# Decay steps of a gated DeltaNet projection stage: other delays between them, and VectorE's and ScalarE's parts kept in program order

## The chip, the cores and the metric

The kernel runs on one core of a Trainium2 chip. The engines of a core work side by side, each through its own queue of instructions in order: TensorE (PE, with its weight loads as PEld), VectorE (DVE), ScalarE (ACT), GpSimd (POOL), and SyncE (SP), which here only issues DMA transfers. The metric is the device time of one execution in microseconds. Three runs of the kernel before took 2248.15, 2249.53 and 2255.58 us; the median is 2249.53.

## The reference

The program is a two-layer encoder trunk over two groups of tokens, 1024 and 256, with a model width of 1024. Layer 0 is two-dimensional neighbourhood attention, layer 1 a bidirectional gated DeltaNet, and a final RMSNorm follows. The change lies in layer 1. After the projection, a five-tap centred depthwise convolution and SiLU, it computes for each of 8 heads and both directions:

```python
g = jnp.cumsum(g.transpose(0, 2, 1).reshape(b, h, n, c), axis=-1)
diff = g[..., :, None] - g[..., None, :]
decay = jnp.where(tril, jnp.exp(jnp.where(tril, diff, 0.0)), 0.0)
k_beta = k * beta[..., None]
a_kk = jnp.where(tril_strict, jnp.einsum('bhncd,bhnsd->bhncs', k_beta, k) * decay, 0.0)
lhs = jnp.eye(c, dtype=jnp.float32) + a_kk
w = lax.linalg.triangular_solve(lhs, k_beta * jnp.exp(g)[..., None], left_side=True,
                                lower=True, unit_diagonal=True)
```

The decay is the exponential of a difference of two cumulative gates, masked to one triangle. It scales the products of keys of a chunk, and the triangular matrix that results has to be inverted.

## The kernel before

The kernel works on chunks of 128 tokens (NB = 10 of them), keeps two 32-bit parts of each projected operand, and so needs three matmuls for a product (`mm<-xh,wh`, `mm<-xl,wh`, `mm<-xh,wl` at L1250). The stage of the change runs from about 770 to 1595 us.

TensorE's main work in it is 32 blocks of 128 channels of q, k and v (L539 copies the result to `raw`) and the blocks of the gate z. A channel block is three PSUM blocks of 512, 512 and 256 tokens with 24 matmuls each, in a pool `mm` of three banks. Each channel block starts a side chain `conv`: ScalarE scales the raw block (L509), VectorE adds four taps (L512, the first kept in program order), ScalarE takes the SiLU (L518, kept in program order; `th`), and SP spills the result. `raw` has two buffers. A z block has a tanh on ScalarE (L563) and one multiplication on VectorE (L554), which frees its bank.

Once a head's k is there, the side chain `invert` of that head begins. In order: TensorE's products of the keys (`pk`, L641); VectorE's norms and the scaling of B (L645 to L649); ScalarE and VectorE take out the diagonal 32x32 blocks into D; VectorE inverts them by substitution (L665 to L673, 60 small operations); two transposes (L677 and L678); ScalarE copies the blocks to M (L686, L687, shown as `X<-D` and `X<-N`) while POOL fills W and WT (L692 to L694). Then there are two rounds in which blocks are joined: L703 on TensorE, L706 on ScalarE, L710 on TensorE, the copies of L712 to L718 on VectorE and ScalarE (two of them transposes into WT), L723, L726, L731 and L733, and SP spills W.

The matrix B of a head, which `invert` starts from, comes from a further side chain, `decays` (L614 to L626). It works on the ten chunks in groups of four, four and two. For each group and each of the two directions a matmul (L605) spreads the cumulative gates into a PSUM bank `t` (three buffers, shared with `pk`), VectorE adds the chunk's other gate and the mask for each chunk (L608, the "taps"), and ScalarE takes the exponential in place (L611). The group's tile E has one buffer. SP spills it to `e_dram` (L624) and POOL adds the two directions into B (L625). The next group's taps can write E only when the spill has read it. `decays` of the next head is put on the list of side chains from within `invert`, after the copies to WT.

The order of the work comes from two places. A side chain is a generator; a list (`Side`) counts the columns that the projection's matmuls have issued, and a chain is taken a step further when its own count is reached: `yield 3500` means 3500 columns later. That sets the order in the program. From it a scheduler makes each engine's queue, and may move instructions ahead of others, except those that `keep_in_program_order` ties. ScalarE has one table of functions loaded at a time; the exponential and the SiLU are in different tables, and `ACT_TABLE_LOAD` stands where it has to be changed.

## Time and profile before

| | |
|---|---|
| median of three runs | 2249.53 us (2248.15 to 2255.58) |
| the profiled execution | 2251.55 us, span 2249.7 us, granted TensorE clock 0.98 |
| TensorE busy | 2166.0 us |
| VectorE busy | 1509.2 us |
| ScalarE busy | 1146.6 us |
| POOL busy | 585.1 us |

The times of the profile count from the start of the span. Rows of a timeline give start, duration, engine, line, operation and tiles, and in brackets how long the engine was idle before it and what ended that. A row of waits gives the waiting engine and line, what it waited for, and the total, the count and the longest. Rows of windows give a stretch and its length, busy time and instructions of PE, PEld, DVE, ACT and POOL, the granted clock, the share of the DMA engines and GB/s.

### The profile page before, as it was taken

To read this page: it belongs to the slowest core of one execution; us is meant where nothing else is said; L and a number is where in the kernel's file an instruction comes from. 1 tells how busy PE (TensorE), PEld (TensorE's weight loads), DVE (VectorE), ACT (ScalarE), POOL (GpSimd) and SP (SyncE) were. 2 spreads that over 40 slices of the span, in tenths; PEclk is the share of its full clock that TensorE was granted. 3 is DMA by queue.
4 is the path that set the end of the run, shared out by engine and by line. 5 is a ranking of instruction groups with operands and counts; after the bars stand their busy time and mean duration, and the time that the engine had idled before them with its cause. 6 is when DMAs were issued, how large, how long until landed. Compare 5 with 4: busy or idle time off the path is not lost.

```text
span 2249.7 us, 34012 instructions
## 1 busy us (share of the span) xinstructions
PE 2166.0 (96%) x12502; PEld 1881.3 (84%) x12502; DVE 1509.2 (67%) x3370; ACT 1146.6 (51%) x2313; POOL 585.1 (26%) x631
## 2 busy tenths in 40 slices
PE   8999999999999999899999999999899999999998
PEld 7789989989878877788888888888788888877887
DVE  5577777776773858768577676867566666675444
ACT  6455545555673454454544546354456666654333
POOL 2100100110230422233132313231176766600000
PEclk9999999999999999899999999999899999999999
DMA  5424342533556343443534444442675566567322
GB/s 181 112 74 118 82 118 75 125 93 97 151 150 182 98 114 89 141 127 101 159 105 134 111 136 115 128 145 71 209 207 164 168 186 180 154 216 234 107 96 85
DMA packets 148456, 300.10 MB, mean 133 GB/s; under 512 B 44976, under 2 KB 67632, under 8 KB 147264
## 3 DMA queue, kind: packets, MB, share of 16 engines
q1 hardware_dynamic: 126784, 232.89, 32.7%
q0 software_dynamic: 12096, 44.05, 11.2%
q10 hardware_dynamic: 9408, 20.98, 3.0%
q8 instruction: 99, 1.62, 0.3%
q14 instruction: 69, 0.57, 0.1%
HBM read 211.92 MB, written 75.45 MB: 128 GB/s over the span
## 4 chain that ended last, share of the span: by engine, by line
PE 70%; DVE 17%; ACT 5%; DMA 4%; issue 3%; POOL 1%; SPq 0%; ACTq 0%; DVEq 0%; POOLq 0%
PE mm L1250 42%; PE mm L1266 4%; DVE tmp L671 3%; DVE X L673 3%; PE k L1014 3%; PE o L986 2%; PE k L1005 2%; PE O L263 2%; PE o L1027 2%; PE u L986 2%; DVE acc L512 2%; PE pt L243 2%; DMA yt<-y_spill 1%; PE t L940 1%; PE S L286 1%
## 5 line engine op out<-in xcount | busy, mean ns | idle before, releaser
L1250 PE MATMUL mm<-xh,wh 128*128 128x512 f32 (+1 forms) x1920 | 700.6, 365 | 6.3 <-DVE z L554 3.2
L1250 PE MATMUL mm<-xh,wl 128*128 128x512 f32 (+1 forms) x1920 | 700.7, 365 | 3.4 <-DMA wl<-w_o 2.2
L1250 PE MATMUL mm<-xl,wh 128*128 128x512 f32 (+1 forms) x1920 | 701.9, 366 | 0.3 <-DVE xl L352 0.2
L1250 PEld LDWEIGHTS mm<-xh,wh 128*128 128x128 f32 x1920 | 367.6, 191 | 52.8 <-DVE z L554 3.8
L1250 PEld LDWEIGHTS mm<-xh,wl 128*128 128x128 f32 x1920 | 367.5, 191 | 47.6 <-DMA wl<-w_o 2.6
L1250 PEld LDWEIGHTS mm<-xl,wh 128*128 128x128 f32 x1920 | 367.7, 191 | 43.1 <-DVE xl L352 0.4
L512 DVE SCALAR_TENSOR_TENSOR acc<-raw,cw,acc 128x1282 f32<-128x1282 f32 x128 | 199.1, 1555 | 4.7 <-ACT acc L509 2.3
L1202 ACT ACTIVATE wh<-wraw 128x1024 fp32r<-128x1024 f32 x92 | 96.8, 1055 | 139.2 <-PE mm L1250 112.7
L1200 POOL CAST wh<-wraw 128x1024 fp32r<-128x1024 f32 x32 | 34.2, 1070 | 498.2 <-PE mm L1250 441.4
L1250 PE MATMUL mm<-yh,wh 128*128 128x512 f32 (+1 forms) x384 | 137.5, 359 | 2.4 <-ACT yh L1124 2.2
L1250 PE MATMUL mm<-yh,wl 128*128 128x512 f32 (+1 forms) x384 | 137.0, 358 | 1.2 <-DVE wl L1204 1.2
L1250 PE MATMUL mm<-yl,wh 128*128 128x512 f32 (+1 forms) x384 | 137.6, 360 | 0.1
L1018 DVE TENSOR_TENSOR vl<-k,vh 128x256 fp32r<-128x256 f32 x160 | 67.1, 424 | 69.6 <-ACT vh L1017 65.1
L247 ACT ACTIVATE ph<-pt 128x512 fp32r<-128x512 f32 (+2 forms) x144 | 67.6, 479 | 77.0 <-PE pt L243 65.3
L539 ACT ACTIVATE raw<-mm 128x512 f32<-128x512 f32 (+1 forms) x96 | 49.9, 522 | 101.9 <-PE mm L1250 96.1
L248 DVE TENSOR_TENSOR pl<-pt,ph 128x512 fp32r<-128x512 f32 (+2 forms) x144 | 75.2, 538 | 38.2 <-ACT ph L247 36.7
L608 DVE SCALAR_TENSOR_TENSOR E<-t,lbG,mask 128x128 f32<-128x128 f32 x160 | 46.9, 342 | 79.7 <-DMA e_spill<-E 78.8
L1206 ACT ACTIVATE wl<-wraw 128x1024 fp32r<-128x1024 f32 x84 | 88.5, 1053 | 16.3 <-DMA wraw<-w_qk 8.4
L221 ACT ACTIVATE P<-P,mx 128x384 f32<-128x384 f32 (+1 forms) x128 | 75.0, 587 | 39.6 <-DVE mx L220 38.3
L1266 PE MATMUL mm<-wh,xl 128*128 128x256 f32 x320 | 91.9, 287 | 0.6 <-POOL xl L65 0.6
L1017 ACT ACTIVATE vh<-k 128x256 fp32r<-128x256 f32 x160 | 60.6, 380 | 62.5 <-PE k L1014 59.3
L1266 PE MATMUL mm<-wl,xh 128*128 128x256 f32 x320 | 91.6, 286 | 0.5 <-DVE wl L1204 0.5
(314 smaller groups left out, 4917.1 us busy)
## 6 DMA issues: line engine op xcount, KB each, us to landing
wraw<-w_qkv SPq DMA_DIRECT2D x32, 512.0 KB, 3.7
qkv_spill<-th SPq DMA_DIRECT2D x32, 512.0 KB, 2.7
wraw<-w_go SPq DMA_DIRECT2D x32, 512.0 KB, 3.6
wl<-w_qkv POOLq DMA_DIRECT2D x30, 512.0 KB, 8.0
Al<-e_spill SPq DMA_DIRECT2D x8, 1280.0 KB, 6.7
qe<-eg_spill SPq DMA_DIRECT2D x16, 640.0 KB, 8.0
wraw<-w_qk SPq DMA_DIRECT2D x16, 512.0 KB, 3.9
wl<-w_qk POOLq DMA_DIRECT2D x16, 512.0 KB, 8.6
```

The lines of the kernel that those rows point to most:

```text
L221: nc.scalar.activation(Pv, Pv, AF.Exp, scale=-1.0, bias=mx[:, 0:1], accum_out=mx[:, 1:2])
L247: nc.scalar.activation(view(ph), view(pt), AF.Copy)
L248: nc.vector.tensor_sub(view(pl), view(pt), view(ph))
L512: tap = nc.vector.scalar_tensor_tensor(acc, r[:, i:i + m], cw[:, f, i:i + 1], acc, op0=OP.mult, op1=OP.add)
L671: nc.vector.tensor_mul(tv, N[:, 0:c, c:c + 1].to_broadcast([128, c, n]), X[:, c:c + 1, c + 1:32].to_broadcast([128, c, n]))
L673: nc.vector.tensor_add(X[:, 0:c, c + 1:32], X[:, 0:c, c + 1:32], tv)
L986: self.tc.nc.tensor.matmul(ps, w[x], v[y], start=(first and i == 0), stop=(i == 2))
L1014: nc.tensor.matmul(pw, W[:, d, cs[d]], Y[d], start=True, stop=True)
L1202: nc.scalar.activation(wh, raw, AF.Copy)
L1206: nc.scalar.activation(wl, raw, AF.Copy, scale=-1.0)
L1250: nc.tensor.matmul(ps, w[:, k, :], x[k][b], start=(k == 0 and i == 0), stop=(k == KD - 1 and i == 2))
L1266: nc.tensor.matmul(ps, x[k][b][:, cc], w[:, k % 4, :], start=(k == 0 and i == 0), stop=(k == KD - 1 and i == 2))
```

## The change

`decay` becomes a generator: the matmul and VectorE's taps are its first step, and the exponential follows 2500 columns later. For all heads but the first, the taps and the exponential are tied in program order. In `decays` the delay after a direction is 3000 columns instead of 3500 (1000 for head 0), and after the spill of the first and the second group there is a further delay of 14000 columns (0 for head 0). In `invert` of head 0, the decays of head 1 are put on the list before the substitution, with a delay of 30000, rather than behind the copies to WT; for heads 1 to 6 the place and the delay of 4000 stay. The delay before L703's matmuls is 42000 columns for head 0, and 34000 as before for the others.

```diff
--- before.py
+++ after.py
@@ -599,16 +599,22 @@
         nc.vector.tensor_scalar(mask[:, d], a["jp"], 0.0, NEG, op0=drop, op1=OP.mult)
 
 
-def decay(nc, a, ap, pool, h, d, c0, n, E, nt=2):
-
+def decay(tc, a, ap, pool, h, d, c0, n, E, nt=2):
+
+    nc = tc.nc
     pg = pool.tile([128, 512], F32, name="t", bufs=nt)
     nc.tensor.matmul(pg[:, :128 * n], a["one_hot"][:, 8 * d + h, None].to_broadcast([128, 128]),
                      a["GR"][:, 128 * c0:128 * c0 + 128 * n], start=True, stop=True)
     for c in range(n):
-        nc.vector.scalar_tensor_tensor(E[:, c], pg[:, 128 * c:128 * c + 128],
-                                       a["lbG"][:, 8 * d + h, c0 + c:c0 + c + 1], a["mask"][:, d],
-                                       op0=OP.add, op1=OP.add)
-    nc.scalar.activation(E, E, AF.Exp)
+        tap = nc.vector.scalar_tensor_tensor(E[:, c], pg[:, 128 * c:128 * c + 128],
+                                             a["lbG"][:, 8 * d + h, c0 + c:c0 + c + 1], a["mask"][:, d],
+                                             op0=OP.add, op1=OP.add)
+        if h:
+            tc.keep_in_program_order(tap)
+    yield 2500
+    exp = nc.scalar.activation(E, E, AF.Exp)
+    if h:
+        tc.keep_in_program_order(exp)
 
 
 def decays(tc, a, ap, pp, h, Bs):
@@ -619,10 +625,12 @@
         n = min(4, NB - c0)
         E = ap.tile([128, 2, 4, 128], F32, name="E", bufs=1)[:, :, :n]
         for d in range(2):
-            decay(nc, a, ap, pp, h, d, c0, n, E[:, d], 3)
-            yield 3500
+            yield from decay(tc, a, ap, pp, h, d, c0, n, E[:, d], 3)
+            yield 3000 if h else 1000
         nc.sync.dma_start(a["e_dram"][h, :, :, c0:c0 + n], E)
         nc.gpsimd.tensor_add(B[:, c0:c0 + n], E[:, 0], E[:, 1])
+        if c0 < 8:
+            yield 14000 if h else 0
     Bs[h] = B
 
 
@@ -649,6 +657,8 @@
             nc.vector.scalar_tensor_tensor(B[:, c0 + c], pk[:, c], a["nrk"][:, h, c0 + c:c0 + c + 1], B[:, c0 + c],
                                            op0=OP.mult, op1=OP.mult)
         yield 2000
+    if h == 0:
+        a["side"].add(decays(tc, a, ap, pp, 1, Bs), 30000)
     sl = [slice(32 * i, 32 * i + 32) for i in range(4)]
     half = [slice(0, 64), slice(64, 128)]
     for s in sl:
@@ -693,11 +703,11 @@
         nc.gpsimd.tensor_copy(W[sl[i], 0, :, q], diag(i, 1 - lo))
         nc.gpsimd.tensor_copy(W[sl[i], 1, :, q], diag(i, lo))
         yield 0
-    if h < 7:
+    if 0 < h < 7:
         a["side"].add(decays(tc, a, ap, pp, h + 1, Bs), 4000)
-    else:
+    elif h:
         factors(tc, a)
-    yield 34000
+    yield 42000 if h == 0 else 34000
     zt = pp.tile([128, NB, 32], F32, name="m", bufs=2)
     for c in range(NB):
         nc.tensor.matmul(zt[:, c], B32[:, c], M[:, c], start=True, stop=True)
```

What the scheduler makes of it is shown at two places, a steady head and the first chain, for two engines each. Lines below 607 keep their numbers; those from L608 on become one to ten larger (the exponential L611 is L615, the transpose L678 is L688, L712 is L722, L723 is L733, L1250 is L1260).

VectorE in a steady head (that of head 2's chain), from the chain's last transpose on; `raw_8851` and `raw_8850` are the two buffers of the convolution's input. Before:

```order
L678 STREAM_TRANSPOSE D<-X 128x32x32
L512 SCALAR_TENSOR_TENSOR acc<-raw_8851,cw,acc 128x1282 x2
L608 SCALAR_TENSOR_TENSOR E<-t,lbG,mask 128x128
L512 SCALAR_TENSOR_TENSOR acc<-raw_8851,cw,acc 128x1282
L608 SCALAR_TENSOR_TENSOR E<-t,lbG,mask 128x128
L512 SCALAR_TENSOR_TENSOR acc<-raw_8851,cw,acc 128x1282
L608 SCALAR_TENSOR_TENSOR E<-t,lbG,mask 128x128 x18
L512 SCALAR_TENSOR_TENSOR acc<-raw_8850,cw,acc 128x1282
L712 STREAM_TRANSPOSE WT<-m 32x10x32
L512 SCALAR_TENSOR_TENSOR acc<-raw_8850,cw,acc 128x1282
```

The same place in the change:

```order
L688 STREAM_TRANSPOSE D<-X 128x32x32
L512 SCALAR_TENSOR_TENSOR acc<-raw_8851,cw,acc 128x1282 x4
L609 SCALAR_TENSOR_TENSOR E<-t,lbG,mask 128x128 x8
L512 SCALAR_TENSOR_TENSOR acc<-raw_8850,cw,acc 128x1282 x4
L609 SCALAR_TENSOR_TENSOR E<-t,lbG,mask 128x128 x8
L722 STREAM_TRANSPOSE WT<-m 32x10x32
L723 STREAM_TRANSPOSE WT<-m 32x10x32
L725 COPY W<-m 32x10x32
L726 COPY W<-m 32x10x32
L512 SCALAR_TENSOR_TENSOR acc<-raw_8851,cw,acc 128x1282 x4
L609 SCALAR_TENSOR_TENSOR E<-t,lbG,mask 128x128 x4
```

The taps now come in groups of eight, eight and four with four convolution taps ahead of each group, where before single taps stood between convolution taps and eighteen together behind them.

ScalarE in the same head, from the raw copy on that follows the copies to M. Before:

```order
L539 ACTIVATE raw_8850<-mm 128x512
L611 ACT_TABLE_LOAD
L611 ACTIVATE E<-E 128x512 x2
L539 ACTIVATE raw_8850<-mm 128x256
L1202 ACTIVATE wh<-wraw 128x1024
L509 ACTIVATE acc<-raw_8850,cw 128x1282
L1206 ACTIVATE wl<-wraw 128x1024
L539 ACTIVATE raw_8851<-mm 128x512
L611 ACTIVATE E<-E 128x512
```

The same place in the change:

```order
L539 ACTIVATE raw_8850<-mm 128x512
L615 ACT_TABLE_LOAD
L615 ACTIVATE E<-E 128x512 x2
L518 ACT_TABLE_LOAD
L518 ACTIVATE th<-acc 128x1282
L539 ACTIVATE raw_8850<-mm 128x256
L1212 ACTIVATE wh<-wraw 128x1024
L509 ACTIVATE acc<-raw_8850,cw 128x1282
L539 ACTIVATE raw_8851<-mm 128x512
```

The convolution's SiLU (`th`) with a table load stands right behind the first group's exponentials now, ahead of the raw copy of 256 columns; the second group's exponentials have moved further back.

VectorE in the first chain (that of head 0), from the last transpose on. Before:

```order
L678 STREAM_TRANSPOSE D<-X 128x32x32
L512 SCALAR_TENSOR_TENSOR acc<-raw_8851,cw,acc 128x1282
L608 SCALAR_TENSOR_TENSOR E<-t,lbG,mask 128x128
L512 SCALAR_TENSOR_TENSOR acc<-raw_8851,cw,acc 128x1282
L608 SCALAR_TENSOR_TENSOR E<-t,lbG,mask 128x128
L512 SCALAR_TENSOR_TENSOR acc<-raw_8851,cw,acc 128x1282
L608 SCALAR_TENSOR_TENSOR E<-t,lbG,mask 128x128
L512 SCALAR_TENSOR_TENSOR acc<-raw_8851,cw,acc 128x1282
L608 SCALAR_TENSOR_TENSOR E<-t,lbG,mask 128x128 x4
L712 STREAM_TRANSPOSE WT<-m 32x10x32
L713 STREAM_TRANSPOSE WT<-m 32x10x32
```

The same place in the change:

```order
L688 STREAM_TRANSPOSE D<-X 128x32x32
L512 SCALAR_TENSOR_TENSOR acc<-raw_8851,cw,acc 128x1282 x4
L609 SCALAR_TENSOR_TENSOR E<-t,lbG,mask 128x128 x4
L512 SCALAR_TENSOR_TENSOR acc<-raw_8850,cw,acc 128x1282
L722 STREAM_TRANSPOSE WT<-m 32x10x32
L512 SCALAR_TENSOR_TENSOR acc<-raw_8850,cw,acc 128x1282
L723 STREAM_TRANSPOSE WT<-m 32x10x32
L512 SCALAR_TENSOR_TENSOR acc<-raw_8850,cw,acc 128x1282
L725 COPY W<-m 32x10x32
L512 SCALAR_TENSOR_TENSOR acc<-raw_8850,cw,acc 128x1282
L554 SCALAR_TENSOR_TENSOR z<-z,mm 128x512
L726 COPY W<-m 32x10x32
```

Sixteen of head 1's twenty taps are ahead of the transpose in the change, nine before. A second convolution's taps (`raw_8850`) now stand around the transposes to WT, and the z multiplication (L554) right behind them.

TensorE in the first chain, around the joining of blocks. Before, L710's ten matmuls stood among the projection's and L723's first ten behind these:

```order
L1250 MATMUL mm<-xh_2_7758,wh 128x256
L1250 MATMUL mm<-xl_2_7782,wh 128x256
L1250 MATMUL mm<-xh_2_7758,wl 128x256
L723 MATMUL m<-WT,B 128x64 x10
L731 MATMUL m<-W,Z 128x64 x10
L1250 MATMUL mm<-xh_0_7735,wh 128x512
L1250 MATMUL mm<-xl_0_7759,wh 128x512
L1250 MATMUL mm<-xh_0_7735,wl 128x512
```

The same place in the change, with L720 for L710 and L733 for L723:

```order
L1260 MATMUL mm<-xh_2_7758,wh 128x256
L1260 MATMUL mm<-xl_2_7782,wh 128x256
L1260 MATMUL mm<-xh_2_7758,wl 128x256
L720 MATMUL m<-X,Z 128x32 x10
L733 MATMUL m<-WT,B 128x64 x10
L1260 MATMUL mm<-xh_0_7735,wh 128x512
L1260 MATMUL mm<-xl_0_7759,wh 128x512
L1260 MATMUL mm<-xh_0_7735,wl 128x512
```

L731's ten matmuls are no longer here, and L720's ten have no projection's rows between them and L733's. On TensorE in a steady head, the fourth decay matmul of a head stands 82 rows behind the first; before it was 35 rows.

## The prediction

> **What bounds the kernel now.** I read the page's busy times and chain of waits first, then TensorE's waits in the projection stage of the gated DeltaNet layer, then the same stage cut at the heads, and last the timelines at one steady stall and at the first chain.
>
> ```profile
> PE 2166.0 (96%) x12502; PEld 1881.3 (84%) x12502; DVE 1509.2 (67%) x3370; ACT 1146.6 (51%) x2313; POOL 585.1 (26%) x631
> PE 70%; DVE 17%; ACT 5%; DMA 4%; issue 3%; POOL 1%; SPq 0%; ACTq 0%; DVEq 0%; POOLq 0%
> ```
>
> TensorE is busy for 96% of the span and carries 70% of the chain that ended last. Time comes off only where TensorE waits or runs at a low clock. In the stage of the change (780 to 1600 us) its waits are few, and the largest is the decays' matmul at L605:
>
> ```profile
> PE t L605 <- DVE E L608: 17.0, 6, 3.3
> ```
>
> It waits for a PSUM bank that VectorE's taps at L608 have not yet read: 17.0 us in six waits, one in the first chain (0.4) and five of up to 3.3. Cut at the first transpose of each head's chain, the stage reads (length, busy times, granted clock, DMA):
>
> ```profile
> 840.42:928.39 87.97, 77.81 (x391) 67.91 (x391) 68.85 (x148) 41.56 (x60) 25.39 (x24) 0.86 0.39 113
> 928.39:1024.39 96.00, 94.78 (x534) 82.16 (x533) 72.64 (x150) 47.92 (x70) 30.17 (x26) 1.00 0.45 126
> 1024.39:1124.79 100.40, 97.09 (x540) 84.69 (x539) 71.58 (x150) 48.42 (x71) 26.11 (x26) 0.98 0.47 127
> 1124.79:1225.21 100.42, 97.11 (x540) 84.71 (x539) 71.62 (x150) 48.43 (x71) 26.14 (x26) 0.98 0.46 126
> 1225.21:1326.56 101.35, 98.02 (x540) 85.42 (x539) 71.62 (x150) 48.42 (x71) 26.12 (x26) 0.97 0.45 124
> 1326.56:1426.80 100.24, 96.94 (x540) 84.61 (x539) 71.57 (x150) 48.43 (x71) 26.11 (x26) 0.98 0.46 126
> 1426.80:1527.20 100.40, 97.08 (x547) 84.76 (x546) 78.61 (x193) 47.43 (x70) 29.80 (x29) 1.00 0.44 122
> ```
>
> The second row is a head without such a stall: 96.00 us at clock 1.00. The next five have one each and take 100.24 to 101.35 us; four of them show 0.97 or 0.98. The first row, with the first chain, shows 0.86. One stall as TensorE sees it:
>
> ```profile
> 1154.30 0.40 PE L605 MATMUL t<-GR,one_hot 128*128 128x512 f32 x1
> 1154.53 0.39 PE L1250 MATMUL mm<-xh,wl 128*128 128x512 f32 x1
> ...
> 1163.38 0.73 PE L605 MATMUL t<-GR,one_hot 128*128 128x512 f32 x1 [3.31 <-DVE E L608]
> ...
> 1164.76 0.63 PE L1250 MATMUL mm<-xl,wh 128*128 128x512 f32 x1
> 1165.19 0.63 PE L1250 MATMUL mm<-xh,wl 128*128 128x512 f32 x1
> ```
>
> Rows of 512 columns start 0.23 us apart at full clock and 0.43 apart after the 3.31 us. VectorE in the same stretch:
>
> ```profile
> 1154.20 2.08 DVE L678 STREAM_TRANSPOSE D<-X 128x1024 f32<-128x1024 f32 x1
> 1156.10 3.17 DVE L512 SCALAR_TENSOR_TENSOR acc<-raw,cw,acc 128x1282 f32<-128x1282 f32 x2
> ...
> 1162.64 1.63 DVE L608 SCALAR_TENSOR_TENSOR E<-t,lbG,mask 128x128 f32<-128x128 f32 x6
> 1168.04 2.16 DVE L608 SCALAR_TENSOR_TENSOR E<-t,lbG,mask 128x128 f32<-128x128 f32 x8 [3.77 <-DMA e_spill<-E]
> 1180.05 1.13 DVE L608 SCALAR_TENSOR_TENSOR E<-t,lbG,mask 128x128 f32<-128x128 f32 x4 [9.85 <-DMA e_spill<-E]
> ```
>
> The chain's last transpose ends at 1156.2; then come convolution taps of 1.55 us each with single decay taps between them. Only at 1162.64 do the taps go together (0.27 us each: eight in 2.16), and the first bank is free at 1163.4. After that VectorE waits for a spill (3.77 and 9.85 us), since E is one tile.
>
> **The change, part by part.** The sum is made against the profiled execution, 2251.55 us (span 2249.7); the median of the runs shown is 2249.53, 2.0 lower.
>
> *The five stalls.* The first two decay matmuls of a head stay where they are. The fourth, which reuses the first one's bank, stands 35 TensorE rows behind the first before, 82 now. VectorE's new order is four convolution taps, then eight decay taps: 1156.2 + 4 x 1.55 + 4 x 0.27 = 1163.5 for the bank, as before. TensorE would without the stall have come to the old place at 1163.38 - 3.31 = 1160.1; 47 rows on (44 of 512 columns at 0.23, three of 256 at half of it) it is 1170.5. The bank is then free 7 us ahead, so it stalls again only if the taps come 7 us later than this. The fifth and sixth, which reuse the second's and the third's, stand another 66 and 78 rows further on. Removed: 17.0 - 0.4 = 16.6 us.
>
> *The clock behind them.* The four heads at a low clock are longer than 96.00 by 4.40, 4.42, 5.35 and 4.24; less 3.3 each, 1.1, 1.1, 2.05 and 0.94 remain, 5.2 us. The fifth (clock 1.00) gives none beyond its stall. Together 21.8, taken as 22. Its lower bound is 16.6 (the clock stays); the upper takes the whole missing clock of the rows, 2 + 2 + 3 + 2 = 9, so 25.6.
>
> *What the new order may cost.* On VectorE nothing is added. On ScalarE each group's exponentials now stand together, and the convolution's Silu between groups brings the other table in: six more table loads in the stage.
>
> ```profile
> L611 ACT ACT_TABLE_LOAD x15 | 19.2, 1283 | 1.4 <-issue 1.2
> 1164.84 0.37 ACT L539 ACTIVATE raw<-mm 128x256 f32<-128x256 f32 x1
> 1173.71 1.27 ACT L518 ACTIVATE th<-acc 128x1282 f32<-128x1282 f32 x1
> ```
>
> 6 x 1.283 = 7.7 us. ScalarE is busy for 48 of a head's 100 us in the rows above, so the loads lie in idle time if none stands ahead of a copy that TensorE waits for. One such copy does move: the 256-column raw copy, at 1164.84 now, goes behind both exponentials, a load and a Silu. Taps done at 1156.2 + 6.2 + 8 x 0.27 = 1164.6; exponential 0.63, load 1.28, Silu 1.27, copy 0.37: drained at 1168.1. Its bank (one of three) is wanted after two further blocks of 24 matmuls x 0.23 = 11.0 us, from about 1160.4 (two rows of 256 columns behind 1160.1): 1171.4. Slack 3.3 us, no cost; with that cover gone, each us beyond it is one of TensorE per head.
>
> *The spill.* SP's issue moves with the last exponential of a group and has nothing new behind it. It lands in 3 us:
>
> ```profile
> e_spill<-E SPq DMA_DIRECT2D x16, 512.0 KB, 3.0
> DVE E L608 <- DMA e_spill<-E: 78.8, 13, 11.8
> ```
>
> Now four convolution taps (6.2 us) and the wait for their first operand stand between a group's taps and the next group's, so most of the 78.8 us should go. Off TensorE's path, it is worth nothing by itself; what it would cost on VectorE is rival E. POOL's addition of the two directions (1.3 us) goes with the exponentials and is next wanted a chain later.
>
> *The first chain.* VectorE, ScalarE and TensorE there:
>
> ```profile
> 881.87 1.89 DVE L678 STREAM_TRANSPOSE D<-X 128x1024 f32<-128x1024 f32 x1
> 886.31 0.47 ACT L686 ACTIVATE X<-N 32x320 f32<-32x320 f32 x1
> 886.92 3.15 PE L703 MATMUL m<-X,B 128*128 128x32 f32 x14 [4.57 <-ACT X L686]
> ...
> 903.13 1.30 PE L723 MATMUL m<-WT,B 128*128 128x64 f32 x10 [0.31 <-POOL Z L714]
> 904.96 1.33 PE L723 MATMUL m<-WT,B 128*128 128x64 f32 x10 [0.53 <-ACT W L718]
> 907.96 4.50 PE L731 MATMUL m<-W,Z 128*128 128x64 f32 x20 [1.67 <-issue]
> 915.10 0.80 PE L1250 MATMUL mm<-xh,wh 128*128 128x512 f32 x1 [2.64 <-DVE z L554]
> ...
> 901.95 0.51 DVE L712 STREAM_TRANSPOSE WT<-m 32x320 f32<-32x320 f32 x1 [10.55 <-PE m L710]
> 914.36 0.68 DVE L554 SCALAR_TENSOR_TENSOR z<-z,mm 128x512 f32<-128x512 f32 x1
> ```
>
> and the windows around it:
>
> ```profile
> 885.00:900.00 15.00, 13.08 (x58) 11.76 (x58) 6.40 (x11) 7.24 (x15) 8.27 (x9) 0.66 0.00 1
> 900.00:925.00 25.00, 19.85 (x106) 18.19 (x105) 16.29 (x46) 11.13 (x16) 4.79 (x5) 0.73 0.56 187
> ```
>
> Its waits are 4.57, 0.31, 0.53, 1.67 and 2.64, 9.7 us in all. Missing clock: 0.34 of 13.1 us and 0.27 of 19.9 us, 4.5 + 5.4 = 9.9. So at most 19.6 us are to be had. Head 1's decays now start ahead of the substitution, and seven more of its taps (7 x 0.27 = 1.9 us) stand before the last transpose: the seventh copy of M, which ended at 886.31 + 0.47, ends at 888.7. TensorE comes to L703's matmuls 13 rows later, 886.92 - 4.57 + 13 x 0.2 (rows of 512 and of 256 columns) = 885.0, and waits 3.7 instead of 4.57. The two transposes to WT (0.51 and 0.52) now have a convolution tap between them and L723's matmuls directly behind L710's: a wait of 0.51 + 1.55 + 0.52 = 2.6 where there were 0.31 and 0.53. Against that, the z operation of L554, which at 914.36 releases TensorE, now stands behind the fourth convolution tap rather than behind L733's copies: with L710's end at its old time, 901.95 + 0.51 + 0.52 + 3 x 1.55 + 0.49 + 0.68 = 908.8 against 915.10, 6.3 us earlier. L731's second half (ten matmuls, 2.2 us of the 4.50) still has to be done later. 6.3 - 2.2: I take 4 us. Below, -4: the 2.6 us wait is new and brings the clock down once more; above, 19.6.
>
> *The last chain* moves its L703 matmuls ten rows forward and its decays some 3 us back; I take 0, from -2 to 3.
>
> Sum: 22 + 4 = 26 us; 2251.55 - 26 - 2.0 = 2223.5, taken as 2224. With the steady term between 19 and 25 and the first chain between 0 and 8 the likeliest case alone runs from 2217 to 2231.
>
> [...] After waits of 1.67 and 2.64 us the first chain shows clock 0.73, and after 3.31 us a steady head shows 0.43 us between matmuls. [...]
>
> **The rivals.**
> B: the first chain is freed wholly, waits and clock. For it: taps and z move forward by several us. Against it: 3.7 and 2.6 us of wait can be read off the new order. 22 + 19.6 = 41.6: 2208.
> B': the first chain keeps waits of 3.7 and 2.6 us but not the low clock behind them, of which half, 5 us, is gone beyond the 4: 26 + 5 = 31, 2218.5. Against it: the 0.73 after short waits.
> C: half of the steady gain is given back. The 3.3 us of slack of the raw copy are short by 2.2 us in each of the five heads, because VectorE starts the four convolution taps late or a table load falls ahead of another raw copy: 26 - 11 = 15, 2234.5. For it: ScalarE is strictly in order and the exponentials are now pinned. Against it: 48% busy.
> D: the stall only changes its place, a bank of three waiting on the next group's taps: the 22 are gone again and the first chain's 4 with them: 2249.
> E, slower: the taps still wait for the spill, as the longest of the 13 waits does (11.8 us), and pinned exponentials hold ScalarE's queue with raw copies behind. The wait less the slack is 11.8 - 3.3 = 8.5 us a head, five heads 43; less 22 gained, 2249.5 + 21 = 2270.5. It decides from a wait of 3.3 + 22/5 = 7.7 us per head. Against it: four convolution taps stand ahead of each group, more than twice the 3 us of a landing.
>
> **How the numbers follow.** The forecast, 2224, has 0.44; B 0.13, B' 0.08, C 0.17, D 0.10, E 0.08. The range 2206 to 2244 holds the forecast, B', C and most of B, and leaves out D and E with a tail of B: two in ten. A measurement of this kernel can tell about 0.3%, 6.7 us. Faster is the forecast, B, B' and C: 0.82; within 0.3% is D, 0.10; slower E, 0.08.
>
> **What would show it.** TensorE's wait for the taps falls from 17.0 to under 2 us; the heads' lengths come to about 96 at clock 1.00; VectorE's wait for the spill falls from 78.8 to under 20; 21 table loads for the exponentials. In the first chain, waits of about 3.7 (before L703's matmuls), 2.6 (before L723's) and 3 (before the projection). It is wrong if TensorE waits for the raw copy (C), for the taps at another place (D), or if the waits for the spill stay (E).

## The result: 25 to 29 us less, and the profile after

The change took 2221.39 us in the median of four runs (2218.22 to 2223.32) against 2250.16 of the kernel before: the ratio is 0.9864, with a 95% interval from 0.9844 to 0.9884. Two later repeats of the same kernel gave 0.9878 (0.9857 to 0.9899) and 0.9882 (0.9864 to 0.9900); the medians differ from those of the kernel before by 28.8, 25.4 and 28.8 us. The profiled execution took 2223.32 us with a span of 2221.5, 28.2 less than the span of before.

TensorE's busy time and, for the stage of the change, TensorE's wait for the taps and VectorE's wait for the spill (total, count, longest):

```profile
PE 2151.7 (97%) x12502; PEld 1871.1 (84%) x12502; DVE 1508.1 (68%) x3370; ACT 1153.9 (52%) x2319; POOL 582.8 (26%) x631
PE t L606 <- DVE E L609: 1.7, 1, 1.7
DVE E L609 <- DMA e_spill<-E: 10.2, 2, 7.7
```

The wait of 17.0 us is 1.7, and the wait for the spill 10.2 instead of 78.8. TensorE is busy 14 us less for the same 12502 matmuls; its granted clock over the whole span is 0.986 against 0.980. Two heads of the stage, cut as before and with the same columns (the rows of 1024.39 and 1124.79 in the kernel before):

```profile
1019.43:1114.49 95.06, 94.25 (x534) 82.37 (x533) 71.59 (x150) 47.94 (x70) 25.67 (x25) 1.00 0.47 130
1114.49:1209.88 95.39, 95.39 (x540) 83.54 (x539) 71.97 (x150) 48.41 (x71) 26.04 (x26) 1.00 0.47 131
```

The next two take 95.43 and 95.39 us. So the four heads that took 100.24 to 101.35 us take 95.06 to 95.43, all at clock 1.00. The prediction's last row (1426.80:1527.20) is left out: the next chain's first transpose stands at 1513.77, so that row is not the length of a head. The head that the prediction showed, on VectorE:

```profile
1145.85 6.48 DVE L512 SCALAR_TENSOR_TENSOR acc<-raw,cw,acc 128x1282 f32<-128x1282 f32 x4
1152.25 2.15 DVE L609 SCALAR_TENSOR_TENSOR E<-t,lbG,mask 128x128 f32<-128x128 f32 x8
```

and the first and the fourth decay matmul on TensorE, neither of which waits:

```profile
1144.04 0.40 PE L606 MATMUL t<-GR,one_hot 128*128 128x512 f32 x1
...
1160.04 0.47 PE L606 MATMUL t<-GR,one_hot 128*128 128x512 f32 x1
```

The first four taps end 1.1 us after 1152.25, so the bank is free at 1153.3 and the matmul comes at 1160.04. At the same place of the program everything here is 10.25 us earlier than in the profile before.

Where the 28 us are is read best from one ScalarE copy that both kernels make at the same places, the raw copy of the projection (L539). Three of them after (the first in the stage, one in head 2's chain, and one behind the last steady head):

```profile
782.82 0.58 ACT L539 ACTIVATE raw<-mm 128x512 f32<-128x512 f32 x1
1031.90 0.60 ACT L539 ACTIVATE raw<-mm 128x512 f32<-128x512 f32 x1 [3.38 <-PE mm L1260]
1500.44 0.60 ACT L539 ACTIVATE raw<-mm 128x512 f32<-128x512 f32 x1 [4.84 <-PE mm L1260]
```

and the same three before:

```profile
783.94 0.58 ACT L539 ACTIVATE raw<-mm 128x512 f32<-128x512 f32 x1
1037.11 0.60 ACT L539 ACTIVATE raw<-mm 128x512 f32<-128x512 f32 x1 [2.35 <-PE mm L1250]
1530.07 0.60 ACT L539 ACTIVATE raw<-mm 128x512 f32<-128x512 f32 x1 [4.84 <-PE mm L1250]
```

Ahead of the stage the change is 1.12 us earlier, at the second copy 5.21, at the third 29.63. So the first chain brought 5.21 - 1.12 = 4.1 us and the steady heads 29.63 - 5.21 = 24.4. The last raw copy of the stage starts at 1548.00 against 1575.90, 27.90 earlier: the last chain lost 1.7 us again. The rest of the program takes 673.5 us after that copy, 673.8 before. The same subtraction for all runs stands in a table further below.

What the 24.4 us were made of can be added up, since both kernels run the same number of matmuls between the second and the third copy. Before, and then the change:

```profile
1037.11:1530.07 492.96, 476.38 (x2644) 415.56 (x2643) 355.69 (x773) 237.97 (x345) 130.44 (x126) 0.98 0.46 125
1031.90:1500.44 468.54, 468.54 (x2644) 410.25 (x2643) 359.37 (x778) 239.07 (x346) 130.00 (x126) 1.00 0.48 131
```

TensorE was idle there for 492.96 - 476.38 = 16.6 us and is never idle now. Behind four of the five stalls its clock was low as well, three times for 3.4 us and once for 6.8, 17.1 us in all. In such a stretch the granted clock is 0.50:

```profile
1163.40:1166.80 3.40, 3.40 (x9) 2.82 (x10) 0.87 (x4) 3.00 (x5) 2.60 (x5) 0.50 0.20 78
```

So 8.5 us of clock were missing, and 16.6 + 8.5 = 25.1 us account for the 24.4 gained to within 0.7.

### The profile page after: what moved, and what is told of

It is laid out like the page before. It is cut to its first block, busy times and chain, and to the rows that moved or that the text cites. A ratio compares the mean times of both kernels' runs of the same rounds, so it can differ in the third digit from the quotient of the medians.

```text
span 2221.5 us, 34043 instructions
## 1 busy us (share of the span) xinstructions
PE 2151.7 (97%) x12502; PEld 1871.1 (84%) x12502; DVE 1508.1 (68%) x3370; ACT 1153.9 (52%) x2319; POOL 582.8 (26%) x631
## 5 line engine op out<-in xcount | busy, mean ns | idle before, releaser
L1260 PE MATMUL mm<-xh,wh 128*128 128x512 f32 (+1 forms) x1920 | 697.5, 363 | 4.2 <-DVE z L554 1.8
L1260 PE MATMUL mm<-xh,wl 128*128 128x512 f32 (+1 forms) x1920 | 697.8, 363 | 3.0 <-DMA wl<-w_o 2.3
L1260 PE MATMUL mm<-xl,wh 128*128 128x512 f32 (+1 forms) x1920 | 699.8, 364 | 0.3 <-DVE xl L352 0.2
L1260 PEld LDWEIGHTS mm<-xh,wh 128*128 128x128 f32 x1920 | 366.0, 191 | 49.1 <-DVE z L554 2.4
L1260 PEld LDWEIGHTS mm<-xh,wl 128*128 128x128 f32 x1920 | 366.0, 191 | 45.8 <-DMA wl<-w_o 2.7
L1260 PEld LDWEIGHTS mm<-xl,wh 128*128 128x128 f32 x1920 | 366.2, 191 | 42.3 <-DVE xl L352 0.4
L1260 PE MATMUL mm<-yh,wh 128*128 128x512 f32 (+1 forms) x384 | 137.4, 359 | 2.0 <-ACT yh L1134 1.9
L1260 PE MATMUL mm<-yh,wl 128*128 128x512 f32 (+1 forms) x384 | 137.0, 358 | 1.2 <-DVE wl L1214 1.2
L1260 PE MATMUL mm<-yl,wh 128*128 128x512 f32 (+1 forms) x384 | 137.6, 359 | 0.3 <-DVE yl L1135 0.3
L539 ACT ACTIVATE raw<-mm 128x512 f32<-128x512 f32 (+1 forms) x96 | 49.7, 520 | 94.4 <-PE mm L1260 92.8
L1276 PE MATMUL mm<-wh,xh 128*128 128x256 f32 x320 | 91.7, 288 | 0.1
```

Of the source, the lines that this page charges most:

```text
L539: nc.scalar.activation(r[:, t0 + o:t0 + o + n], ps, AF.Copy)
L1260: nc.tensor.matmul(ps, w[:, k, :], x[k][b], start=(k == 0 and i == 0), stop=(k == KD - 1 and i == 2))
L1276: nc.tensor.matmul(ps, x[k][b][:, cc], w[:, k % 4, :], start=(k == 0 and i == 0), stop=(k == KD - 1 and i == 2))
```

## The experiments

The theory was that the distance on TensorE between the first and the fourth decay matmul removes the stall, and that the landing of the spill and the ties in program order matter only as far as they set that distance or hold up a raw copy. The rivals were the ties and the spill.

### The ties taken away

```diff
-        if h:
-            tc.keep_in_program_order(tap)
...
-    if h:
-        tc.keep_in_program_order(exp)
```

> The delays of the change alone: the ties in program order (VectorE's taps, ScalarE's exponential) are taken away, everything else is as in the change. Theory (the distance on TensorE between the first and the fourth decay matmul of a head is what removes the stall): the fourth matmul still stands more than 60 rows behind the first, the first four taps still end at about the same time, so TensorE's wait for the taps stays under 2 us and the time is that of the change, 2221 us, from 2217 to 2226. Rival (the ties carry the gain, since without them single taps slip between convolution taps): the waits for the taps come back to about 10 us or more and the time is 2235 us or longer.

Measured: 2227.37 us (2225.24 to 2229.96), ratio 0.9897 (0.9881 to 0.9912). In the steady heads there is no wait for the taps, and they gain 24.4 us as in the change. The time is 1.4 us beyond the upper end of what was expected, and most of the difference lies in one place, the first chain:

```profile
895.18 4.44 PE L709 MATMUL m<-X,B 128*128 128x32 f32 x20 [5.35 <-ACT X L692]
...
934.25 0.79 PE L1256 MATMUL mm<-xh,wh 128*128 128x512 f32 x1 [2.91 <-DVE z L554]
893.00:908.00 15.00, 12.82 (x51) 11.88 (x51) 5.35 (x4) 10.30 (x16) 7.38 (x8) 0.57 0.24 90
```

The rows are two of TensorE's waits there and the window around the first. The wait ahead of the joining matmuls is 5.35 us, one of 1.99 us for a decay matmul and one of 2.91 for the z operation follow; the clock falls to 0.57. The ties do nothing for the steady heads. They are worth some 5 to 8 us in the first chain (+1.3 against -3.4 to -6.3 in three executions of the change, in the table of all runs); which instruction moves there was not followed further.

### The old delays, with the ties kept

```diff
-    yield 2500
+    yield 0
...
-            yield 3000 if h else 1000
+            yield 3500
...
-            yield 14000 if h else 0
+            yield 0
```

> The ties alone: delays between the decay steps as in the kernel before (3500 columns after a direction, none after a group, the exponential right behind its taps), first chain as in the change. Theory (distance): the fourth decay matmul is back at about row 40, TensorE reaches it at about 1161 of the steady head shown and the bank is free at 1163.5, a wait of 2.3 us; the sixth waits for the second group's taps, which wait for the spill, about 1 us. With the clock behind it some 4.4 us a head, so the steady gain is lost: 2243 us, from 2238 to 2250, with 10 to 20 us of waits for the taps. Rival (the ties do it): 2221 us.

Measured: 2250.24 us (2248.14 to 2254.12), ratio 0.9995 (0.9984 to 1.0006): no difference from before at all.

```profile
PE t L606 <- DVE E L609: 20.2, 9, 3.2
DVE E L609 <- DMA e_spill<-E: 81.1, 12, 11.2
1159.21 0.55 PE L606 MATMUL t<-GR,one_hot 128*128 128x512 f32 x1 [3.00 <-DVE E L609]
1055.00:1070.00 15.00, 12.13 (x46) 9.98 (x46) 5.89 (x18) 9.06 (x11) 5.82 (x8) 0.77 0.40 105
1458.00:1473.00 15.00, 11.80 (x60) 9.76 (x61) 6.00 (x18) 11.18 (x13) 6.46 (x9) 1.00 0.47 130
```

The rows are the waits of TensorE and VectorE in the stage, one stall, and the windows behind the first and the last stall. The stall is back with 3.0 to 3.2 us a head, all of it at the fourth matmul rather than 2.3 and 1 at two places, and the clock falls to 0.77 behind the first of them and not at all behind the last. Head 2's decays have a stall too (2.30 us at 959.70), which the expectation did not count. The steady gain is not merely smaller but gone: 0.8 us are lost there. The time is at the upper end of what was expected. The first chain is still 2.8 us shorter than before; the total shows nothing of it, since from the last steady head to the end this execution takes 3.8 us more.

### Only the delay after a group taken away

```diff
-            yield 14000 if h else 0
+            yield 0
```

> The change with the 14000 columns after a group's spill set to 0, ties and the other delays kept. The fourth decay matmul stands at row 48 and the sixth at row 74; sixteen taps stand together, so the second group's wait for the first group's spill again. Theory (distance): the fourth matmul comes at 1163.1 against a bank free at 1163.5, 0.4 us; the sixth at about 1169.4 against 1170, 0.3 us; VectorE's waits for the spill are back at 20 us or more but cost TensorE only what stands here: 2225 us, from 2221 to 2230. Rival (the landing of the spill ahead of the next group is what counts): the 24 us are lost, 2240 us or longer, and if the exponentials hold up the raw copies, above 2250.

Measured: 2224.95 us (2223.10 to 2231.05), ratio 0.9894 (0.9876 to 0.9912).

```profile
DVE E L609 <- DMA e_spill<-E: 32.8, 8, 7.7
1146.62 0.47 PE L606 MATMUL t<-GR,one_hot 128*128 128x512 f32 x1 [1.01 <-DVE E L609]
1144.00:1159.00 15.00, 13.99 (x77) 11.77 (x76) 11.15 (x20) 12.42 (x18) 7.46 (x9) 1.00 0.36 129
```

The rows are VectorE's wait for the spill, one stall and the window behind it. VectorE waits 32.8 us for the spill, three times as long as in the change, and TensorE pays a single wait of 1.0 us in each of five heads, at the fourth matmul; the expected wait of the sixth is there in one head only, 0.41 us. In these heads the clock stays at 1.00. So the landing of the spill ahead of the next group is not what brings the gain. But the steady heads gain 17.7 us instead of 24.4, and the total is hardly longer than the change's, because the first chain gains 11.3 us instead of 4.1. That was not expected and led to the runs on head 1 below.

### The first chain as before

```diff
-    if h == 0:
-        a["side"].add(decays(tc, a, ap, pp, 1, Bs), 30000)
...
-    if 0 < h < 7:
+    if h < 7:
...
-    yield 42000 if h == 0 else 34000
+    yield 34000
```

> The change with its first-chain part undone: head 1's decays are put on the list behind the copies, and 34000 columns stand before the joining matmuls of head 0 too. Theory: the first-chain part is worth what the same raw copies show in the two profiles, 4 us: 2225 us, from 2222 to 2229, with the wait before the joining matmuls of the first chain back at about 4.6 us. Rival (the first chain's waits only change place): 2221 us, no difference.

Measured: 2230.30 us (2225.99 to 2233.98), ratio 0.9913 (0.9897 to 0.9930).

```profile
881.40 0.61 PE L711 MATMUL m<-X,B 128*128 128x32 f32 x2 [4.49 <-ACT X L694]
...
1027.48 0.67 PE L1258 MATMUL mm<-xh,wh 128*128 128x512 f32 x1 [4.48 <-DVE z L554]
```

The wait ahead of the joining matmuls is 4.49 us, as before the change, and a new wait for the z operation of 4.48 us stands at 1027.48. By the raw copies the first chain is 0.1 us longer than before, where the change made it 4.1 shorter, and the steady heads gain 24.5. The time is 1.3 us beyond the upper end of what was expected. In the medians the difference from the change is 4 to 9 us, depending on which of the change's three medians it is taken against.

### The first-chain part alone, on the kernel before

```diff
+    if h == 0:
+        a["side"].add(decays(tc, a, ap, pp, 1, Bs), 30000)
...
-    if h < 7:
+    if 0 < h < 7:
...
-    yield 34000
+    yield 42000 if h == 0 else 34000
```

> The kernel before with the first-chain part of the change alone (head 1's decays on the list ahead of the substitution, 42000 columns before head 0's joining matmuls). Theory (the two parts of the change add up): 4 us faster than before, 2247 us, with the five stalls of 3.3 us as they were. Rival (the first chain's part helps only together with the ties and delays of head 1's decays): 2251 us or longer.

Measured: 2252.48 us (2247.68 to 2258.56), ratio 1.0006 (0.9993 to 1.0019). The rival holds. By the raw copies the first chain is only 1.5 us shorter, less than the 2.9 us by which three executions of the change differ there, and head 2's decays, which had no stall, now have one:

```profile
892.95 1.84 PE L705 MATMUL m<-X,B 128*128 128x32 f32 x10 [3.50 <-ACT X L688]
...
964.56 0.47 PE L605 MATMUL t<-GR,one_hot 128*128 128x512 f32 x1 [2.37 <-DVE E L608]
1166.58 0.77 PE L605 MATMUL t<-GR,one_hot 128*128 128x512 f32 x1 [3.31 <-DVE E L608]
```

The two parts do not add up: alone, the first-chain part is worth next to nothing; with the ties and the new delays of head 1's and head 2's decays it is worth 3.5 us or more (+0.1 without it, -3.4 to -6.3 with it).

### Head 1 without the delay after a group

```diff
-            yield 14000 if h else 0
+            yield 14000 if h > 1 else 0
```

> The change itself, unaltered, beside the three other kernels on the same chip: 2221 us, from 2217 to 2226. It is the measure for the others.

> The change with the 14000 columns after a group taken away for head 1 alone (heads 2 to 7 keep them). In the run without any group delay the stretch up to the first raw copy of head 2's chain was 7 us shorter than in the change, and the steady heads 1.2 to 1.7 us longer. Theory (the two are separate: the delay helps the steady heads and hurts the first chain): 7 us faster than the change, 2214 us, from 2210 to 2218, and the steady heads at 95.4 us as in the change. Rival (the 7 us came from the order of the steady heads' decays too): 2221 us.

Measured side by side: the change 2226.60 us (2218.09 to 2227.48), this kernel 2218.56 (2215.29 to 2219.43), ratio 0.9848 (0.9834 to 0.9863) against before. By the raw copies the first chain gains 10.4 us and the steady heads 24.5; so the delay helps the steady heads and hurts the first chain. The time is 0.6 us beyond the upper end of what was expected. The first chain's waits and clock in this kernel:

```profile
864.80 0.47 PE L606 MATMUL t<-GR,one_hot 128*128 128x512 f32 x1 [1.95 <-DVE E L609]
895.24 2.39 PE L713 MATMUL m<-X,B 128*128 128x32 f32 x20 [0.44 <-ACT X L696]
901.71 4.48 PE L720 MATMUL m<-X,Z 128*128 128x32 f32 x20 [3.53 <-ACT Z L716]
893.00:908.00 15.00, 11.02 (x66) 10.45 (x66) 13.98 (x13) 11.70 (x17) 14.42 (x11) 0.71 0.38 141
908.00:923.00 15.00, 15.00 (x81) 13.12 (x80) 13.63 (x45) 4.74 (x11) 5.57 (x3) 0.95 0.34 81
```

and in the change:

```profile
878.98 0.35 PE L606 MATMUL t<-GR,one_hot 128*128 128x256 f32 x1 [1.73 <-DVE E L609]
889.15 1.05 PE L713 MATMUL m<-X,B 128*128 128x32 f32 x8 [1.84 <-ACT X L696]
903.23 2.37 PE L733 MATMUL m<-WT,B 128*128 128x64 f32 x10 [2.83 <-POOL B L631]
906.62 2.40 PE L733 MATMUL m<-WT,B 128*128 128x64 f32 x10 [1.02 <-ACT Z L736]
888.00:903.00 15.00, 11.25 (x67) 11.04 (x67) 9.35 (x11) 10.11 (x16) 9.88 (x9) 0.72 0.18 65
903.00:918.00 15.00, 13.74 (x64) 12.25 (x65) 8.96 (x30) 5.41 (x9) 0.92 (x2) 0.71 0.46 134
```

The waits shown sum to 5.9 us here and 7.4 in the change. In these windows the clock is low for 10.2 us here and for 17.1 in the change.

> The kernel without the group delay for head 1 once more, to see whether it is faster than the change beyond the spread of both. Theory: the first chain's waits are 2.5 us fewer and its stretch of low clock is half as long, so 4 to 7 us less than the change in the same call, about 2217 us. Rival (the difference of the last comparison was spread): within 2 us of the change.

> The change, unaltered, as the measure for the run beside it: between 2218 and 2227 us.

Measured side by side once more: this kernel 2219.92 us (2216.74 to 2222.25), the change 2222.72 (2219.76 to 2228.88); ratios against before 0.9864 (0.9846 to 0.9882) and 0.9882 (0.9864 to 0.9900). The difference is 8.0 us the first time and 2.8 the second, of the same sign, with intervals that overlap; 2.8 lies between the theory's 4 to 7 and the rival's 2. That the version beats the kernel before is plain; that it beats the change is supported by the first chain, 7.0 us shorter in the first pair of traces and 5.0 in the second, and not settled by the times. The theory's second half failed: the low stretch of the chain is not half as long in the second pair (13.7 us here, 10.2 in the change). What is less in both pairs is TensorE's idle time, as the second table below shows.

### Head 7 later

```diff
-    yield 42000 if h == 0 else 34000
+    yield 42000 if h == 0 else 46000 if h == 7 else 34000
```

on top of the kernel of the section before.

> As the run before with, for head 7, 46000 columns in place of 34000 before its first joining matmuls (L713). In the change TensorE waits 4.4 us there and its clock is 0.87 to 0.89 for the next 30 us. Theory (there are enough rows of the projection left to fill the 4.4 us): that wait falls under 1 us and the time by 4 to 8 us more, 2208 us, from 2204 to 2213. Rival (the last chain is what the next stage waits for, so that a later start only moves the wait): 2214 us or longer, with longer waits behind 1570 us.

Measured: 2222.77 us (2220.59 to 2224.86), ratio 0.9871 (0.9855 to 0.9888); it missed.

```profile
1523.62 3.10 PE L713 MATMUL m<-X,B 128*128 128x32 f32 x16 [4.44 <-issue]
1575.00:1650.00 75.00, 64.00 (x366) 54.93 (x365) 44.81 (x103) 40.70 (x105) 43.89 (x53) 0.86 0.66 183
```

The rows are the wait ahead of L713's matmuls and a window of the next stage. In the change that wait is 4.42 us at 1526.49, and the clock over the 30 us from 1526 on is 0.83, where the expectation has 0.87 to 0.89. The wait is still 4.44 us: the scheduler left L713's matmuls at the same TensorE row and moved only the later joins. Up to the stage's last raw copy the last chain is 3.0 us shorter, where the kernel without this edit loses 0.3; but that is no gain, since the twenty joining matmuls of L733 now stand behind the copy. From that copy to the end the kernel takes 679.4 us against 673.3, with a clock in the stretch shown of 0.86 against

```profile
1575.00:1650.00 75.00, 65.05 (x394) 56.02 (x392) 48.07 (x109) 42.42 (x114) 47.23 (x56) 0.93 0.69 198
```

0.93. Both stretches together are 2.1 to 2.9 us longer than in the two executions without the edit, no more than the 3.4 us by which three executions of the change differ there. So the edit brings nothing; whether it costs something is not shown. The spill of head 7's W lands later (1560.23 against 1555.42), but the next stage's first load of it starts only 0.4 us later (1568.34 against 1567.92).

### A stall of 2 us

```diff
-            yield 3000 if h else 1000
+            yield 1900 if h else 1000
...
-            yield 14000 if h else 0
+            yield 0
```

> No group delay, and 1900 columns in place of 3000 after a direction: the fourth decay matmul stands at row 43, five rows ahead of the run without a group delay, so that TensorE should wait 1.0 + 5 x 0.23 = 2.1 us in each of five heads. The question is what a wait of 2 us costs beyond itself. A wait of 1.0 cost a head 1.25 us against the change, one of 3.0 cost 3.7 to 6.0. Theory (the clock falls behind a wait from about 2 us on): heads 3 to 4 us longer than the change's 95.4, 2237 us. Rival (only waits of about 3 us and more bring it down): heads 2.1 to 2.5 us longer, clock 1.00, 2230 us.

Measured: 2246.27 us (2244.35 to 2252.53), ratio 0.9975 (0.9962 to 0.9987).

```profile
1161.64 0.48 PE L606 MATMUL t<-GR,one_hot 128*128 128x512 f32 x1 [2.08 <-DVE E L609]
1159.00:1174.00 15.00, 12.22 (x64) 9.86 (x63) 5.71 (x18) 10.62 (x13) 6.88 (x9) 1.00 0.34 123
```

The rows are one stall and the window around it. The fourth matmul waits 2.08 us, as worked out, and the sixth 0.7, which was not. Against the change a head is 3.2 to 3.6 us longer for 2.8 to 3.2 us of waits, and the clock stays at 1.00 in all five: the length is the theory's, the clock the rival's. So in these heads a wait of 2 us costs little beyond itself. One of 1.95 us in head 1's decays (862.31), in the same execution, did bring the clock down (0.89 over the next 15 us). The total is longer than either theory had it, because the first chain gains only 1.8 us here, where the run without the group delay gained 11.3.

### The ledger of all runs

Shift against the kernel before between the same raw copies, in us (minus is shorter): from the first of the stage to the one in head 2's chain (783.94 and 1037.11 before), from there to the one behind the last steady head (1530.07), from there to the stage's last (1575.90), and from 1530.07 to the end of the program.

| kernel | first chain | steady heads | last chain | last chain and rest |
|---|---|---|---|---|
| the change | -4.1 | -24.4 | +1.7 | +1.5 |
| the change again | -3.4 | -24.4 | +1.9 | +3.2 |
| the change, third | -6.3 | -24.4 | +1.9 | -0.2 |
| ties away | +1.3 | -24.4 | +1.3 | +3.2 |
| old delays | -2.8 | +0.8 | -3.3 * | +3.8 |
| no delay after a group | -11.3 | -17.7 | +1.1 | +4.0 |
| first chain as before | +0.1 | -24.5 | +0.3 | +1.3 |
| first-chain part alone | -1.5 | +1.3 | -0.6 | 0.0 |
| head 1 without the delay | -10.4 | -24.5 | +0.3 | -0.2 |
| head 1 without, repeated | -11.3 | -24.5 | +0.9 | +0.5 |
| and head 7 later | -11.7 | -24.4 | -3.0 * | +2.6 |
| a stall of 2 us | -1.8 | -7.2 | +1.5 | +2.1 |

In the two rows with a star the twenty matmuls of L733 of head 7's chain stand behind the last raw copy, in the others ahead of it; their last chain is not comparable.

What stands ahead of the stage is from 2.7 us shorter to 5.4 us longer than in the kernel before, although nothing was changed there; that is why the columns tell more than the medians do.

The first two stretches hold the same matmuls, shape by shape, in every kernel. So their length can be split: TensorE's idle time, the missing clock (half of the time at a granted clock of 0.50), and what is left.

| kernel | first chain: length | idle | missing clock | steady heads: length | idle | missing clock |
|---|---|---|---|---|---|---|
| before | 253.2 | 12.7 | 15.4 | 493.0 | 16.6 | 8.5 |
| the change | 249.1 | 13.4 | 10.2 | 468.5 | 0 | 0 |
| the change again | 249.8 | 12.8 | 11.9 | 468.5 | 0 | 0 |
| the change, third | 246.9 | 13.0 | 8.5 | 468.5 | 0 | 0 |
| ties away | 254.5 | 12.9 | 17.1 | 468.5 | 0 | 0 |
| old delays | 250.4 | 15.2 | 10.2 | 493.8 | 15.4 | 10.2 |
| no delay after a group | 241.9 | 8.7 | 8.5 | 475.3 | 5.4 | 0 |
| first chain as before | 253.3 | 15.6 | 11.9 | 468.5 | 0 | 0 |
| first-chain part alone | 251.7 | 14.2 | 11.9 | 494.2 | 16.6 | 10.2 |
| head 1 without the delay | 242.8 | 8.1 | 10.2 | 468.5 | 0 | 0 |
| head 1 without, repeated | 241.9 | 10.0 | 6.8 | 468.5 | 0 | 0 |
| and head 7 later | 241.5 | 9.2 | 6.8 | 468.6 | 0 | 0 |
| a stall of 2 us | 251.4 | 14.4 | 11.9 | 485.7 | 14.5 | 0 |

What is left is 224.4 to 225.7 us of the first chain in all thirteen. Of the steady heads it is 467.4 to 468.6, and 469.9 and 471.2 in the two kernels with waits of 1 and 2 us. So what the kernels differ by is idle time and clock.

## Why the prediction was right

*The five stalls.* Right, step by step. Forecast with the head's own 10.25 us of shift taken off: the bank free at 1163.5 - 10.25 = 1153.25, measured 1153.3; the fourth matmul at 1170.5 - 10.25 = 1160.25, measured 1160.04. The 7 us of slack are there. That the distance is the cause and not the ties or the spill is shown by three runs: with the ties and without the distance nothing is gained; with the distance and without the ties all of the steady gain is there; and without the delay after a group the stall shrinks with the distance to 1.0 us. Counted in the traces, 35, 39, 43, 48 and 88 matmuls from the first to the fourth went with waits of 3.3, 3.0, 2.1, 1.0 and 0 us. (The 82 rows that the prediction goes by are these 88 with six pairs of L713's small matmuls as one row each.)

*The clock behind the stalls.* The mechanism was right, the term too small: stalls and clock were forecast at 16.6 + 5.2, taken as 22 us, and 24.4 were gained, of which 16.6 are the stalls and 7.8 are left for the clock. The heads do not return to 96.00 but to 95.06 to 95.43. The row of 96.00 that served as the measure held three short waits on TensorE of its own,

```profile
935.43 0.50 PE L1250 MATMUL mm<-xh,wh 128*128 128x512 f32 x1 [0.51 <-DVE z L554]
941.86 0.50 PE L1250 MATMUL mm<-xh,wh 128*128 128x512 f32 x1 [0.34 <-ACT raw L539]
970.27 0.50 PE L1250 MATMUL mm<-xh,wh 128*128 128x512 f32 x1 [0.38 <-ACT raw L539]
```

1.23 us in all, so it was no clean head. It also holds 534 matmuls, where the four heads compared with it hold 540. The waits made it too long and the missing matmuls too short; in sum each difference was taken some 0.6 to 0.9 us too small.

*The raw copy behind the exponentials.* Forecast to be drained at 1168.1 - 10.25 = 1157.85:

```profile
1155.08 1.28 ACT L518 ACT_TABLE_LOAD   x1
1156.37 1.28 ACT L518 ACTIVATE th<-acc 128x1282 f32<-128x1282 f32 x1
1157.56 0.36 ACT L539 ACTIVATE raw<-mm 128x256 f32<-128x256 f32 x1
```

It ends at 1157.9. No block waited for it in the steady heads, where TensorE is never idle, and rivals C, D and E did not come. Six more table loads came, but as 18 ahead of the exponentials and 19 ahead of the SiLU (15 and 16 before), not as 21 of the former: of the sign that was to show it, the sum held and the split did not.

*The first chain.* Forecast 4 us, measured 4.1, and 3.4 and 6.3 in the two repeats. The number came out by luck; the mechanism did not hold. The 4 us were to come from TensorE's waits, by an earlier z operation, with the low clock as it was. Before, and then the change, over the whole stretch:

```profile
783.94:1037.11 253.17, 240.44 (x1258) 204.47 (x1257) 185.31 (x412) 125.41 (x186) 76.39 (x77) 0.94 0.41 117
782.82:1031.90 249.08, 235.67 (x1257) 201.18 (x1257) 184.93 (x412) 130.23 (x190) 74.00 (x77) 0.96 0.43 120
```

TensorE's idle time is 12.7 us before and 13.4 after (12.8 and 13.0 in the repeats), so the waits brought nothing. What fell is the missing clock, from 15.4 us to 10.2, 11.9 and 8.5. In the profiled execution 1.7 of the 5.1 us lie ahead of the chain, where the clock is low for 6.8 us at 794.8 before and for 3.4 at 833.3 in the change. The single waits are not those of the forecast either. The wait ahead of the joining matmuls is 1.84 us, not 3.7; that ahead of L733 (L723 before) is 2.83 for 2.6; the 3 us for the z operation are 1.02 for the copies to Z and 0.97 for z; and a wait of 1.73 for a decay matmul (878.98) was not foreseen. So of B' the clock term came (5 us forecast; 5.1, 3.4 and 6.8 measured), and not the 4 us of waits beside it. Those 5 us were half of the 9.9 worked out from the windows before; that half would go was an estimate that no row of that profile shows. Shorter waits alone did not free the clock: with none above 2.9 us it is still 0.72 from 888 to 903 us and 0.71 from 903 to 918. Why the same waits kept the clock low for 17.1 us in two executions and for 10.2 in the third stays open.

*The last chain.* Forecast 0 with bounds of -2 and 3; it lost 1.7 us. Its wait grew from 4.10 to 4.42 us, which is 0.3 of it. Two more matmuls of 512 columns stand ahead of the last raw copy (99 against 97), which by the rows shown is 0.5 to 0.9 us; what took the rest was not found.

The whole came to 26.8 us in the stage, where 26 were forecast.

## What to carry to other kernels

When an engine waits for a buffer of a small ring, look first at how many of its own instructions lie between the use of a buffer and its next use, and lengthen that distance to more than the consumer's delay; a tie that fixes the consumer's order does not do it. Judge such an edit by the same instruction in both traces, place by place: a delay that helped the steady heads cost the first chain 5 to 7 us, and the medians showed only the sum. Over a stretch with the same matmuls, split the length into idle time and missing clock before a gain is put down to either: here a forecast of 4 us came true through the clock, while the waits that it rested on had not shrunk. A head that is to serve as the measure of an undisturbed one should have its own short waits taken off first.

## What the runs showed of the hardware

TensorE's clock fell behind a wait more often the longer the wait was; no single length divides the two cases. Taken are waits of TensorE for a decay matmul with no longer wait beside them and the clock at 1.00 ahead of them. Of eight waits of 0.96 to 1.73 us none brought the clock down. Of fifteen of 1.95 to 2.37 us four did: 859.29 in the kernel without the group delay, 862.31 in that with the stall of 2 us, 864.80 in that without head 1's delay, and 964.56 in that with the first-chain part alone (0.89 over the next 15 us each). Of fifteen of 3.0 to 3.35 us, in the five heads of three kernels, twelve did (0.77 to 0.89). The same wait of head 1's decays, 1.99 us without the group delay and 1.97 in the repeat without head 1's delay, went both ways:

```profile
859.00:874.00 15.00, 14.71 (x65) 12.39 (x66) 14.61 (x28) 6.24 (x9) 2.30 (x2) 0.89 0.44 107
861.00:876.00 15.00, 13.48 (x66) 11.34 (x67) 14.63 (x29) 6.34 (x9) 2.88 (x2) 1.00 0.40 107
```

Behind these waits the clock was low for 3.4 us or for 6.8. In the kernel before, with waits of 3.30 to 3.33 us, it was low for 3.4 us behind the stalls at 1062.94, 1163.38 and 1365.10, for 6.8 behind the one at 1263.80, and not at all behind the one at 1465.40. What decides between these cases the runs do not show. In the first chain of the change, where matmuls with 32 or 64 columns stand next to the waits (L713, L720, L733), waits of 1.84 and 2.83 us went with a clock of 0.72 (888 to 903 us). Whether the small matmuls have a part in that was not tried.
